# The channels of two SSD groups, projected ahead of the attention by seven products of quarters

## The chip, the cores and the metric

The kernel runs on one core of a Trainium2 chip. The metric is the device time of one execution in microseconds (us). Work is spread over five engines with queues of their own: PE multiplies matrices, ACT (ScalarE) evaluates functions and copies, DVE (VectorE) and POOL (GpSimd) do elementwise work, and SP issues most of the transfers between DRAM and on-chip memory. Each engine takes its instructions strictly in the order in which the program lists them, and waits by semaphores for the others.

## The reference

One layer of a hybrid decoder over 1024 tokens of width 1024, in float32 (cut to what matters here):

```python
h = rms_norm(x, norm_mix_g)
proj = h @ w_in                       # z 2048 | xbc 3072 | dt 32 | q_a 256 | kv_a 128 | k_rope 32 | gates 2048
xbc = silu(causal_depthwise_conv(xbc, conv_w, conv_b))     # 4 taps over the tokens
xs, bm, cm = split(xbc, [2048, 2048 + 4 * 128])            # xs, B and C: 4 groups each
dt = softplus(dt_raw + dt_bias)
y_ssd = rms_norm((ssd_chunked_scan(xs * dt, -dt * exp(a_log), bm, cm) + xs * d_skip) * silu(z)) @ w_ssd_proj
y_mla = mla(rms_norm(q_a), rms_norm(kv_a), k_rope) @ w_mla_proj        # 16 heads, causal
x = x + (sigmoid(g0) * y_ssd + sigmoid(g1) * y_mla) @ w_o
u = causal_depthwise_conv(rms_norm(x) @ w_up, conv_ffn_w, conv_ffn_b)  # 3 taps
x = x + (silu(u[:, :2816]) * u[:, 2816:]) @ w_down
```

## The kernel before

A float32 product is made of three matmuls on rounded parts: each operand is split into a high part and a remainder, and `mm3` (L173 to L177) issues high by high, high by low and low by high. So a step of 128 rows of the contraction costs three matmuls of 128x512, and a tile of 128 output columns for all 1024 tokens costs 2 halves x 8 steps x 3 = 48. The high part is cast by ACT, the remainder subtracted by DVE or POOL (`split`, `load_w`, L152 to L171).

The stages follow each other so:

- **Start.** For each half of 512 tokens, the normalised input is transposed in 8 blocks of 128 columns (`tps`), each split into an `h` tile (L263, L264), and multiplied by the 448 small columns (dt, q_a, kv_a, k_rope) into four banks `bl`, which are copied to `sm` (L417). Squares of q_a and kv_a are summed on ACT (L419, L420).
- **Into the attention.** Inverse roots of the means (`rsqrt_mean`, L114 to L125: small DVE operations, two chains), the scaling of `sm` (L433), six transposes of it into `qah`/`qal`/`kvh`/`kvl` (L442 to L447), the rotary tables on POOL (`tabs`, L451; `rq`/`rk`, L459 to L462; `krr`, L469 to L474), the softplus of dt (L480 on) and its running sums over the tokens (L502 to L522).
- **Attention**, four heads at a time. The order of PE is the order of the program, and its own products are short chains through DVE and ACT, so products that have nothing to do with it are put between: the list `background` holds generators, each of which yields once per step of three matmuls. `fill()` (L217) takes as many steps as the next character of the table `PACE` says. In the background are 16 gate tiles (`gate_tile`, stored to `g_d`) and 11 of the 16 z tiles (`z_tiles`, to `z_d`). `flush()` at the end runs what is left.
- **SSD**, four groups. A group's channels are 6 tiles: 4 of xs, one of B, one of C. `conv_tile` projects one with 48 matmuls, adds the 4 taps (one ACT operation, three DVE operations `L812` of 128x1024) and applies silu as tanh (L816, L817). Group 0 is projected alone (`conv_group(0)`); group g+1 fills the gaps of group g, `advance(n)` of 106 to 128 steps per group. A step of the scan is a chunk of 128 tokens: `xp`, `sp`, `yp`, `sn`.
- **Merge** with the gates, w_o, and the **MLP**. Its up projection works on pairs of column tiles: the 2 x 2 quarters (column tile by half of the contraction) against the 2 x 2 quarters of the activations (half of the contraction by half of the tokens) take seven products of sums of quarters in place of eight, of 4 steps each: 84 matmuls a pair and not 96. The sums of weight quarters are made on POOL (`w_sums`, L1149 to L1152), the casts on ACT, the remainders on POOL and DVE (L1141). The order in a pair is: `p5`, `p6`, `p7`, `p3`, `p4` and then `p12` of the next pair, 12 matmuls each and 24 in `p12`. `both_sums` (L1324, DVE) reads the bank of `p5` before `p3` accumulates onto it; it needs the copy of the bank of `p6` by ACT (L1318).

The tile framework releases on-chip memory by pools: the first user of a new pool over old memory waits for the last readers of the old one, transfers among them.

## Time and profile before

| | us |
|---|---|
| three runs | 2224.29, 2228.82, 2230.35: median 2228.82 |
| the profiled execution | 2224.44 |
| its span from the first to the last instruction | 2222.6 |
| PE busy in it | 2173.7 |
| end of the start (last `bl`) | 67.75 |
| first attention product (`s`) | 103.11 |
| attention's last store | 697.05 |
| group 0 projected alone | about 728 to 800 |

Marks of stages are read from the timeline. PE is the engine that is busy nearly always; matmuls overlap, so their pace is read from the distance of their starts and not from the duration of one. The mean granted TensorE clock is 0.996 of full speed.

### The profile page before, as it was taken

Reading aid. Unit: us, or ns where it says so; the run is one execution under the profiler, and the core shown is the slowest. Engines: PE = TensorE matmul, PEld = TensorE weight load, DVE = VectorE, ACT = ScalarE, POOL = GpSimd, SP = SyncE. Lnnn points to the kernel's source line nnn. Section 1 sums busy time; section 2 is a strip of 40 time slices with the busy share of each in tenths; the row PEclk is TensorE's granted clock in tenths of the full one; section 3 lists DMA queues with packets and bytes.
Section 4 is the critical chain, followed back from the end, with each engine's and each line's share of the span. In section 5 each row is a group of like instructions: output and inputs, shape, how many; then the busy total and the mean of one; then the engine's idle time right before and its main releaser. Section 6 shows DMA issues by size and latency. Waiting matters only on the chain.

```text
span 2222.6 us, 31323 instructions
## 1 busy us (share of the span) xinstructions
PE 2173.7 (98%) x11488; PEld 1765.2 (79%) x11488; DVE 1430.4 (64%) x2496; ACT 1012.4 (46%) x1852; POOL 822.4 (37%) x911
## 2 busy tenths in 40 slices
...
GB/s 146 54 68 49 40 48 63 50 45 39 69 43 130 68 76 152 181 162 167 95 227 207 178 223 203 166 162 95 67 95 86 81 81 86 76 142 246 201 130 67
DMA packets 112714, 253.57 MB, mean 114 GB/s; under 512 B 13168, under 2 KB 19248, under 8 KB 112560
## 3 DMA queue, kind: packets, MB, share of 16 engines
...
q8 instruction: 90, 1.47, 0.3%
q14 instruction: 64, 0.52, 0.1%
...
## 4 chain that ended last, share of the span: by engine, by line
PE 75%; DVE 13%; ACT 4%; DMA 3%; issue 2%; POOL 1%; SPq 0%; DVEq 0%; ACTq 0%; POOLq 0%
PE lin L175 12%; PE lin L177 12%; PE lin L176 12%; PE dps L177 8%; PE dps L175 8%; PE dps L176 8%; PE pv L670 2%; PE s L175 2%; PE s L176 1%; PE s L177 1%; PE s L627 1%; PE yp L891 1%; PE sn L874 1%; DMA wraw<-in_w_ssd 1%; DVE qk L588 1%
## 5 line engine op out<-in xcount | busy, mean ns | idle before, releaser
L175 PE MATMUL lin<-h,whi 128*128 128x512 f32 x1440 | 592.4, 411 | 0.0
L177 PE MATMUL lin<-h,wlo 128*128 128x512 f32 x1440 | 564.0, 392 | 0.0
L176 PE MATMUL lin<-h,whi 128*128 128x512 f32 x1440 | 563.0, 391 | 0.0
L175 PEld LDWEIGHTS lin<-h,whi 128*128 128x128 f32 x1440 | 271.4, 188 | 81.6 <-issue 33.4
L177 PEld LDWEIGHTS lin<-h,wlo 128*128 128x128 f32 x1440 | 270.7, 188 | 59.8 <-DVE wlo L154 0.2
L176 PEld LDWEIGHTS lin<-h,whi 128*128 128x128 f32 x1440 | 271.9, 189 | 53.2 <-issue 7.0
L153 ACT CAST whi<-wraw 128x512 fp32r<-128x512 f32 x276 | 166.6, 619 | 281.4 <-PE lin L176 131.6
L154 POOL TENSOR_TENSOR wlo<-wraw,whi 128x512 fp32r<-128x512 f32 x134 | 192.1, 1450 | 185.1 <-ACT whi L153 177.6
L659 ACT ACTIVATE e<-s 128x512 f32<-128x512 f32 (+1 forms) x192 | 93.7, 493 | 164.6 <-DVE s L657 137.7
L664 POOL TENSOR_TENSOR acc<-acc,e 128x512 f32<-128x512 f32 (+3 forms) x80 | 79.6, 995 | 230.8 <-ACT e L659 217.7
L154 DVE TENSOR_TENSOR wlo<-wraw,whi 128x512 fp32r<-128x512 f32 x142 | 99.2, 714 | 94.4 <-ACT whi L153 94.3
L154 DVE TENSOR_TENSOR h<-ar,h 128x1024 fp32r<-128x1024 f32 x40 | 48.7, 1225 | 108.8 <-ACT h L153 108.7
L850 ACT ACTIVATE seg<-abc,acum 128x128 f32<-128x128 f32 x256 | 80.6, 392 | 48.3 <-PE yp L891 42.3
L153 ACT CAST h<-ar 128x1024 fp32r<-128x1024 f32 x40 | 42.1, 1056 | 124.8 <-PE lin L176 115.7
L176 PE MATMUL dps<-wlo,h 128*128 128x512 f32 x240 | 93.4, 389 | 0.0
L175 PE MATMUL dps<-whi,h 128*128 128x512 f32 x240 | 93.4, 389 | 0.0
L177 PE MATMUL dps<-whi,h 128*128 128x512 f32 x240 | 93.4, 389 | 0.0
L812 DVE SCALAR_TENSOR_TENSOR xg<-craw,cl,xg 128x1024 f32<-128x1024 f32 x48 | 73.8, 1537 | 27.4 <-ACT xg L810 26.9
L664 DVE TENSOR_TENSOR acc<-acc,e 128x512 f32<-128x512 f32 (+3 forms) x80 | 53.5, 668 | 41.0 <-ACT e L659 40.4
L1140 ACT CAST xhi<-ur 128x512 fp32r<-128x512 f32 (+1 forms) x41 | 34.1, 832 | 89.5 <-PE dps L176 79.5
L670 PE MATMUL pv<-e,vt 128*64 128x512 f32 (+3 forms) x384 | 72.9, 499 | 0.0
L175 PE MATMUL s<-qh,kh 97*128 97x512 f32 (+1 forms) x192 | 68.5, 357 | 2.0 <-ACT qh L644 1.1
...
## 6 DMA issues: line engine op xcount, KB each, us to landing
wraw<-in_w_main SPq DMA_DIRECT2D x112, 256.0 KB, 3.1
ur<-in_w_up SPq DMA_DIRECT2D x44, 512.0 KB, 3.5
ar<-a_d SPq DMA_DIRECT2D x40, 512.0 KB, 5.1
abc<-ac_d POOLq DMA_DIRECT2D x32, 512.0 KB, 5.2
...
a_d<-uc SPq DMA_DIRECT2D x22, 512.0 KB, 2.6
...
```

Of the source, the lines that this page charges most:

```text
L153: S.copy(hi, raw)
L154: (eng or V).tensor_sub(lo, raw, hi.bitcast(F32))
L175: PE.matmul(ps, lhsT=ah, rhs=bh, start=first, stop=False, **more)
L176: PE.matmul(ps, lhsT=ah, rhs=bl, start=False, stop=False, **more)
L177: PE.matmul(ps, lhsT=al, rhs=bh, start=False, stop=last, **more)
L588: V.tensor_tensor(qk[:, :, 2 + hd, 0:64], qk[:, :, 2 + hd, 0:64], rr[:, :, 2 + hd:3 + hd].broadcast_to([P, 4, 64]), op=ALU.mult)
L659: S.activation(e[:, c0:512], ps[:, 0:w], AF.Exp)
L664: (V if hd else G).tensor_tensor(accs[hd][:, c0:512], accs[hd][:, c0:512], e[:, c0:512], op=ALU.add)
L670: PE.matmul(pv[hd * 64:(hd + 1) * 64, c0:512], lhsT=vt[:, j, hd * 64:(hd + 1) * 64], rhs=es[hd][:, c0:512], start=first, stop=last)
L812: V.scalar_tensor_tensor(c, raw[:, k:k + T], col(cw + k), c, op0=ALU.mult, op1=ALU.add)
L850: S.activation(seg[:, hd, :], abc[:, hd, :], AF.Relu, bias=acum[:, c, 8 * g + hd:8 * g + hd + 1], scale=-1.0)
L1140: S.copy(hi, r)
```

## The change

The 12 tiles of groups 0 and 1 (xs 0 to 7, B 0 and 1, C 0 and 1) are projected between the start and the attention, as six pairs of seven products, with the functions that served the MLP (moved to the top of the program, otherwise the same). The four combinations of activation quarters are made during the second half of the start and behind it (`job`). Each channel is convolved, silu is taken directly, and the result goes to `c_d` in DRAM; the SSD loads it (`channels`). Since the memory is tight, the first half's unsplit `h` (4 of 8 blocks) waits in `h_d` and is split again behind the last pair. The inverse roots, the scaling of `sm` and the softplus move into the gaps of the pairs. The 0.5 that served silu by tanh is now in the weights of the convolution, scaled for groups 2 and 3 behind the pairs. The background of the attention begins with 12 z tiles, then the 16 gates, and what is left of it when the attention ends fills the SSD; the head of `PACE` is shorter, and group 2 joins the fill of the first two groups. PE issues 72 fewer matmuls of 128x512 (7084 for 7156), and as many of every other shape as before. DVE has 61 more instructions, ACT 24 more (4 of them loads of function tables), POOL 15 more, SP 16 more transfers.

```diff
@@ PACE @@
-    "30030000000000000g080212018000011100522073110011303000010111011001011111000010000100001000002000"
+    "2222221116000011100522073110011303000010111011001011111000010000100001000002000"
...
+    c_d = dram.tile([24 * P, T], F32, name="c_d")
+    h_d = dram.tile([P, 4, 512], F32, name="h_d")
...
+    def w_sums(q, t=None):
+        q.s = t or pools["sum"].tile([P, KD, P], F32, name="us", bufs=1)
+        G.tensor_tensor(q.s[:, 0:4, :], q.r2[:, 0:4, :], q.r2[:, 4:8, :], op=ALU.add)
+        G.tensor_tensor(q.s[:, 4:8, :], q.s[:, 0:4, :], q.r1[:, 0:4, :], op=ALU.subtract)
+        G.tensor_tensor(q.r2[:, 0:4, :], q.r1[:, 0:4, :], q.r2[:, 0:4, :], op=ALU.subtract)
+        G.tensor_tensor(q.r1[:, 4:8, :], q.r1[:, 4:8, :], q.s[:, 4:8, :], op=ALU.subtract)
...
+    def product(ps, hl, c0, name, first, last):
+        hi, lo = hl
+        for i in range(4):
+            b = BQ[name][i]
+            mm3(ps, (hi[:, c0 + i, :], lo[:, c0 + i, :]), (b[:, 0, :], b[:, 1, :]), first and i == 0, last and i == 3,
+                skip_group_check=True)
+            yield True
+    def p12(q, x=None, y=None):
+        q.x = x or lin_tile()
+        q.y = y or banks_of[0]()
+        yield from product(q.x, q.a, 0, "11", True, True)
+        yield from product(q.y, q.a, 4, "21", True, True)
...
+    def p6(q, sums=True):
+        drain([product(q.x, q.b, 4, "t2", False, True)])
+        q.s2 = lt.tile([P, 512], F32, name="lt")
+        S.copy(q.s2, q.x)
+        if sums:
+            both_sums(q)
+    def both_sums(q):
+        q.q = lt.tile([P, 512], F32, name="lt")
+        V.tensor_tensor(q.q, q.z, q.s2, op=ALU.add)
+    def p7(q):
+        q.y = banks_of[0]()
+        drain([product(q.y, q.c, 0, "t3", True, True)])
...
-    background += [gate_tile(c) for c in range(16)] + [z_tiles(c) for c in range(11)]
+    background += [z_tiles(c) for c in range(12)] + [gate_tile(c) for c in range(16)]
...
+    cpairs = []
+    for a, c in ((16, 20), (0, 1), (2, 3), (17, 21), (4, 5), (6, 7)):
+        q = Pair()
+        q.pad, q.first, q.ct, q.src = 3, 1, (a, c), (w_main[16 + a], w_main[16 + c])
+        cpairs.append(q)
+    q = cpairs[0]
...
+                    if k == 5:
+                        nc.gpsimd.dma_start(out=h_d, in_=xb[0][:, :, 0:512])
+                else:
+                    if k == 0:
+                        q.s = quad_w()
+                        w_sums(q, q.s)
+                    n = k - 1
+                    if 0 <= n < 4:
+                        job("t1", n, b[1, n], act_tile(), b[0, n], b[1, n])
+                        job("t3", n, b[0, n], quad(), b[0, n + 4], b[0, n])
+                    elif n >= 4:
+                        V.tensor_tensor(b[1, n - 4], b[0, n], b[1, n - 4], op=ALU.subtract)
+                    if k == 3:
+                        w_second(q)
+                    if k > 3:
+                        small_squares(0, k - 4, 1)
                 if k:
-                    if half:
-                        fill()
                     small(half, k - 1, banks)
-            if half:
...
+    def channel(q, kind, u):
+        ct = q.ct[kind]
+        c = cb.tile([P, T], F32, name=f"uc{kind}")
+        cw = CG_CONVW + 4 * ct
+        S.activation(c, u[:, 3:T + 3], AF.Identity, bias=col(CG_CONVB + ct), scale=col(cw + 3))
+        for k in range(3):
+            V.scalar_tensor_tensor(c, u[:, k:k + T], col(cw + k), c, op0=ALU.mult, op1=ALU.add)
+        S.activation(c, c, AF.Silu)
+        nc.sync.dma_start(out=c_d[ct * P:(ct + 1) * P, :], in_=c)
...
+    for i in range(4):
+        job("t2", i, b[1, i], ca.tile([P, 2, 512], F32R, name="tb", bufs=4))
+    low()
+    q.x, q.y = lin_tile(), lin_tile()
+    drain([p12(q, q.x, q.y)])
+    first_sum(q)
+    w_third(q)
+    w_fourth(q)
+    for i in range(4):
+        job("t4", i, b[1, i + 4], quad(), b[1, i + 4], b[1, i])
+    low()
+    xctx.close()
+    cb = cvctx.enter_context(tc.tile_pool(name="cb", bufs=1))
...
+    for j, q in enumerate(cpairs):
+        nx = cpairs[j + 1] if j + 1 < len(cpairs) else None
+        if nx:
+            w_raw(nx)
+            w_first(nx)
+        p5(q)
+        if nx:
+            w_sums(nx)
+        p6(q)
+        if nx:
+            w_second(nx)
+        else:
+            for k in range(4):
+                raw = lt.tile([P, 512], F32, name="lt")
+                nc.sync.dma_start(out=raw.rearrange("p (i c) -> p i c", c=P), in_=h_d[:, :, k * P:(k + 1) * P])
+                h[0][k] = act_tile()
+                split(raw, h[0][k][:, 0, :], h[0][k][:, 1, :])
+        p7(q)
+        c22(q)
+        p3(q)
+        channel(q, 0, q.ug)
+        if nx:
+            w_fourth(nx)
+        p4(q)
+        c21(q)
+        channel(q, 1, q.uv)
+        if nx:
+            w_third(nx)
+            drain([p12(nx)])
+            c11(nx)
+        if j == 0:
+            name = last(mybir.EngineType.Activation)
+            small_squares(1, 0, 1)
+            tc.add_manual_dep(first_square[0], name, mybir.DependencyInfo(
+                mybir.DependencyClass.NoSync, mybir.DependencyReason.DATA), reason="order")
+            small_squares(1, 1, 3)
+        if j == 1:
+            rsqrt_mean(rr[:, 0, :], ss[:, 0, :], 256)
+            rsqrt_mean(rr[:, 1, :], ss[:, 1, :], 128)
+        if j == 2:
+            for half in range(2):
+                ts_ = slice(4 * half, 4 * half + 4)
+                V.tensor_tensor(sm[:, ts_, 32:288], sm[:, ts_, 32:288],
+                                rr[:, 0, ts_].unsqueeze(2).broadcast_to([P, 4, 256]), op=ALU.mult)
+                V.tensor_tensor(sm[:, ts_, 288:416], sm[:, ts_, 288:416],
+                                rr[:, 1, ts_].unsqueeze(2).broadcast_to([P, 4, 128]), op=ALU.mult)
+        if j == 3:
+            v, e, u = cdec, dte, acum
+            name = last(mybir.EngineType.DVE)
+            V.tensor_tensor(v, sm[:, :, 0:32], cl[:, CG_DTB:CG_DTB + 32].unsqueeze(1).broadcast_to([P, NT, 32]),
+                            op=ALU.add)
+            behind(name)
+            V.tensor_scalar(e, v, -1.0, None, op0=ALU.mult)
+            V.tensor_tensor(e, e, v, op=ALU.min)
...
+    G.tensor_scalar(cl[:, CG_CONVW:CG_CONVB + 24], cl[:, CG_CONVW:CG_CONVB + 24], 0.5, None, op0=ALU.mult)
...
         attention()
-        flush()
...
+        def channels(g):
+            chan[g] = dp.tile([P, 4, T], F32, name=f"xg{g % 2}", bufs=1)
+            for n in (16, 20):
+                chan[n + g] = dp.tile([P, T], F32, name="chan", bufs=4)
+            for half in range(2):
+                s = hs_(half)
+                for n in (16, 20):
+                    nc.sync.dma_start(out=chan[n + g][:, s], in_=c_d[(n + g) * P:(n + g + 1) * P, s])
+                nc.sync.dma_start(out=chan[g][:, :, s],
+                                  in_=c_d[4 * g * P:4 * (g + 1) * P, s].rearrange("(j p) t -> p j t", p=P))
...
+        channels(0)
         abc_load(0)
+        z_load(0)
         ls = dp.tile([P, P], F32, name="bt")
         lv = l_d.rearrange("r (c t) -> (r c) t", t=P)
-        for n, _ in enumerate(conv_group(0)):
-            if n == 17:
-                nc.sync.dma_start(out=ls, in_=lv)
-            if n == 33:
-                name = last(mybir.EngineType.DVE)
-                V.reciprocal(ls, ls)
-                behind(name)
-                nc.sync.dma_start(out=lv, in_=ls)
-        later()
-        z_load(0)
-        background.append(z_tiles(11))
+        nc.sync.dma_start(out=ls, in_=lv)
+        channels(1)
+        craws += [dp.tile([P, T + 3], F32, name="craw") for _ in range(2)]
+        for raw in craws:
+            G.memset(raw[:, 0:3], 0.0)
+        advance(12)
+        V.reciprocal(ls, ls)
+        advance(8)
+        nc.sync.dma_start(out=lv, in_=ls)
+        background += [z_tiles(12), z_tiles(13), conv_group(2)]
         fins = []
         for g in range(GROUPS):
-            if g + 1 < GROUPS:
-                background += [conv_group(g + 1), z_tiles(*((12,), (13,), (14, 15))[g])]
-            else:
+            if g == GROUPS - 2:
+                background += [conv_group(3), z_tiles(14, 15)]
+            if g == GROUPS - 1:
                 background += [mla_tiles()]
-            advance(8 if g else 14)
-            n = (106, 104, 128, 112)[g]
+            advance(8)
+            n = (96, 92, 128, 112)[g]
```

Three places show how the order moves. **First**, ACT at the second pair (`uc` is a channel, `us` and `ur` are sums and raw weights of a pair, `lt` a copy of a bank, `sm` the small columns). Before, the squares stood behind the start, among the gates:

```order
L419 ACTIVATE ljunk,lss<-sm 128x256
L420 ACTIVATE ljunk,lss<-sm 128x128
L292 ACTIVATE lt<-lin,hgb 128x512
L419 ACTIVATE ljunk,lss<-sm 128x256
L420 ACTIVATE ljunk,lss<-sm 128x128
L484 ACTIVATE de<-de 128x256
L153 CAST whi<-wraw 128x512
```

Now the second half's squares stand between the casts of the second pair and the copy that `both_sums` needs (the last row):

```order
L309 CAST whi<-us 128x1024
L309 CAST xhi_819<-ur_739 128x512
L309 CAST xhi_843<-ur_740 128x1024
L633 ACTIVATE uc_836<-row_736,cl 128x1024
L358 COPY lt<-lin 128x512
L491 ACTIVATE lt,lss<-sm 128x256
```

```order
L636 ACT_TABLE_LOAD
L636 ACTIVATE uc_812<-uc_812 128x1024
L493 ACTIVATE lt,lss<-sm 128x128
L491 ACTIVATE lt,lss<-sm 128x256
L493 ACTIVATE lt,lss<-sm 128x128
L491 ACTIVATE lt,lss<-sm 128x256
L493 ACTIVATE lt,lss<-sm 128x128
L309 CAST whi<-ur_888 128x1024
L636 ACTIVATE uc_836<-uc_836 128x1024
L309 CAST whi<-us 128x1024
L371 COPY lt<-lin 128x512
```

Eight squares, a table load and two silus have come in ahead of that copy.

**Second**, ACT's queue with the load of the rotary tables. Before, it was issued in the start:

```order
L153 CAST whi<-wraw 128x512
L263 ACTIVATE h<-tps,cl 128x512 x6
L451 DMA tabs<-in_cons 128x256
L497 ACTIVATE ea<-cl 128x32
L417 COPY sm<-bl 128x448
```

Now it is issued behind the last channel's silu:

```order
L758 ACTIVATE kvh<-tps,cl 128x512
L636 ACTIVATE uc_1586<-uc_1586 128x1024
L792 COPY acum<-tps 128x256
L763 DMA tabs<-in_cons 128x256
L796 COPY tot<-tps 128x256
```

Its memory lies over that of the channels, so it waits for the last two stores to `c_d` as well.

**Third**, SP behind the attention. Before:

```order
L681 DMA at_d<-ao 128x512
L685 DMA l_d<-e 4x256
L1070 DMA bt<-l_d 128x128
L988 DMA rb<-at_d 128x512
L307 DMA z_d<-lt 128x512
```

Now the loads of two groups' channels (6 MB) stand between the attention's last store and the next gate stores and weights:

```order
L967 DMA at_d<-ao 128x512
L971 DMA l_d<-e 4x256
L162 DMA wraw<-in_w_main 128x512
L1091 DMA chan<-c_d 128x512 x2
L1092 DMA xg_8312<-c_d 128x4x512
L1091 DMA chan<-c_d 128x512 x2
L1092 DMA xg_8312<-c_d 128x4x512
L1364 DMA bt<-l_d 128x128
L1091 DMA chan<-c_d 128x512 x2
L1092 DMA xg_8327<-c_d 128x4x512
```

```order
L1091 DMA chan<-c_d 128x512 x2
L1092 DMA xg_8327<-c_d 128x4x512
L430 DMA g_d<-lt 128x512 x3
L1373 DMA l_d<-bt 128x128
L162 DMA wraw<-in_w_main 128x512
```

The stores of gates and the weights of the next tile are now behind twelve loads.

391 lines of the change are left out of this document (196 added, 195 removed).

## The prediction

> **What bounds the kernel now.** First the page: busy times, and the shares of the chain that ended last.
>
> ```profile
> PE 2173.7 (98%) x11488; PEld 1765.2 (79%) x11488; DVE 1430.4 (64%) x2496; ACT 1012.4 (46%) x1852; POOL 822.4 (37%) x911
> PE 75%; DVE 13%; ACT 4%; DMA 3%; issue 2%; POOL 1%; SPq 0%; DVEq 0%; ACTq 0%; POOLq 0%
> ```
>
> PE is busy for 2173.7 of 2222.6 us, so only about 49 us of waiting is left, and a matmul less is worth its pace wherever PE doesn't wait. Next the view of windows (us from the start, busy time with the number of instructions of PE, its weight loads, DVE, ACT and POOL, then granted clock, DMA share and GB/s), for the stages that the change touches.
>
> ```profile
> 30.00:60.00 30.00, 30.00 (x163) 27.06 (x162) 9.33 (x14) 15.88 (x37) 8.11 (x9) 1.00 0.17 53
> 60.00:90.00 30.00, 26.91 (x124) 22.83 (x123) 20.43 (x55) 10.99 (x31) 9.04 (x16) 0.94 0.13 42
> 704.00:712.00 8.00, 8.00 (x37) 6.60 (x37) 0.69 (x1) 5.46 (x14) 3.07 (x3) 1.00 0.98 356
> 728.00:800.00 72.00, 72.00 (x320) 59.60 (x319) 33.95 (x27) 27.36 (x39) 17.53 (x14) 1.00 0.21 64
> ```
>
> Group 0's projection alone (728 to 800) has no idle time: moving it saves no wait there, only the matmuls that it drops. The start is full too (30 to 60). What waits is the way into the attention (60 to 90, clock 0.94). Its timeline on PE (start, duration, instruction, idle time before it):
>
> ```profile
> 67.75 0.39 PE L175 MATMUL lin<-h,whi 128*128 128x512 f32 x1
> ...
> 78.43 0.39 PE L177 MATMUL lin<-h,wlo 128*128 128x512 f32 x1
> 81.91 1.94 PE L442 MATMUL tps<-cn,sm 128*128 128x128 f32 x8 [3.09 <-DVE rsa L123]
> 83.50 0.78 PE L175 MATMUL lin<-h,whi 128*128 128x512 f32 x1
> 84.92 0.42 PE L175 MATMUL lin<-h,whi 128*128 128x512 f32 x1
> ...
> 103.11 0.25 PE L175 MATMUL s<-wqh,qah 128*128 128x192 f32 x1
> ```
>
> The 48 starts from 67.75 to 78.43 give the pace: 10.68 / 47 = 0.2272 us a matmul. Then PE waits 3.09 us for the inverse roots, and what follows is slow: the three matmuls from 83.50 to 84.92 take 1.42 us and not 0.68, and the eight transposes before them 1.59. About 1.5 us is lost to the clock on top of the wait. From 67.75 to the first `s` at 103.11 are 35.4 us; the 114 background matmuls in it (25.9 us at the pace) and its transposes and sums (some 4 us) leave about 5.4 us of stall in all.
>
> **The sum, part by part.** It is made against the profiled execution, 2224.44 us, which lies at the low end of the three runs and 4.4 below their median.
>
> *Matmuls dropped.* 72 x 0.2272 = **-16.4**. The pairs of the MLP show what seven products cost with their surroundings; the issues of its weight loads are one pair apart:
>
> ```profile
> 1727.75 4.45 SPq L1127 DMA_DIRECT2D ur<-in_w_up  x2
> 1747.02 4.45 SPq L1127 DMA_DIRECT2D ur<-in_w_up  x2
> ```
>
> 19.27 us for 84 matmuls, where the pace gives 19.08. So 6 x 0.2 = **+1.1**, if the six new pairs run like those. They differ in three things: three convolution taps and not two, chains of the attention put between, and a first pair whose operands are just being made. For these I need durations (groups by line; the number behind the bar is busy us, then mean ns):
>
> ```profile
> L1141 POOL TENSOR_TENSOR wlo<-us,whi 128x1024 fp32r<-128x1024 f32 x19 | 47.5, 2498 | 13.1 <-ACT whi L1140 13.1
> L1149 POOL TENSOR_TENSOR us<-ur 128x512 f32<-128x512 f32 x21 | 29.4, 1400 | 54.8 <-DMA ur<-in_w_up 53.3
> L1151 POOL TENSOR_TENSOR ur<-ur,ur 128x512 f32<-128x512 f32 x22 | 32.3, 1470 | 0.0
> L1152 POOL TENSOR_TENSOR ur<-ur,us 128x512 f32<-128x512 f32 x21 | 44.8, 2132 | 2.7 <-DVE h L1141 1.2
> L154 DVE TENSOR_TENSOR h<-lt,h 128x512 fp32r<-128x512 f32 x16 | 10.7, 688 | 4.5 <-ACT h L153 4.5
> L1141 DVE TENSOR_TENSOR xlo<-ur,xhi 128x512 fp32r<-128x512 f32 x21 | 34.9, 1660 | 0.0
> L1141 DVE TENSOR_TENSOR xlo<-ur,xhi 128x1024 fp32r<-128x1024 f32 x20 | 25.3, 1263 | 0.0
> L1344 DVE SCALAR_TENSOR_TENSOR uc<-uv,cl,uc 128x1024 f32<-128x1024 f32 x44 | 58.9, 1339 | 1.2 <-ACT uc L1342 0.4
> L812 DVE SCALAR_TENSOR_TENSOR xg<-craw,cl,xg 128x1024 f32<-128x1024 f32 x48 | 73.8, 1537 | 27.4 <-ACT xg L810 26.9
> L433 DVE TENSOR_TENSOR sm<-sm,lrr 128x1024 f32<-128x1024 f32 x2 | 2.4, 1218 | 0.0
> L486 DVE RECIPROCAL du<-du 128x256 f32<-128x256 f32 x1 | 1.8, 1753 | 0.0
> L1140 ACT CAST whi<-us 128x1024 fp32r<-128x1024 f32 x21 | 22.2, 1055 | 82.1 <-PE lin L176 79.2 <-POOL us L1150 2.9
> L1342 ACT ACTIVATE uc<-uv,cl 128x1024 f32<-128x1024 f32 x22 | 27.5, 1250 | 18.0 <-DVE uv L1359 14.2 <-DVE uc L1363 3.8
> L1353 ACT ACTIVATE uc<-uc 128x1024 f32<-128x1024 f32 x22 | 23.4, 1064 | 2.1 <-DVE uc L1344 2.1
> L1353 ACT ACT_TABLE_LOAD x1 | 1.3, 1283 | 0.0
> ```
>
> *Second half of the start.* It loses its fill, and DVE gets four more operations of 0.69 in each of four blocks, some 3.5 us with the block's own remainder, where PE has 12 matmuls and 4 transposes, about 2.9. Nothing (the operations lag behind without hurting) to 4 (DVE slowed by POOL's sums beside it, as in the 1.66 of a 128x512 against 0.69); I take **+2**.
>
> *Hand-over from the first pair to the second.* Count from S, the end of the start. DVE has nine remainders, four differences and the first pair's two weight remainders to do: 9 x 0.69 + 4 x 0.69 + 1.26 + 0.69 = 10.9, and is through at about S+12.4 with the casts ahead. Only then is the memory of `xt` free, and the raw weights of the second pair can be loaded. Loads and stores take:
>
> ```profile
> ur<-in_w_up SPq DMA_DIRECT2D x44, 512.0 KB, 3.5
> a_d<-uc SPq DMA_DIRECT2D x22, 512.0 KB, 2.6
> ```
>
> The load lands at 15.9, the cast ends at 17.0, POOL's remainder at 19.4, its four sums (1.40, 1.40, 1.47, 2.13) at 25.8, the remainder of the sums at 28.3. PE, with 108 matmuls from S on, wants that remainder at about 25. So it waits 3.3, and by the 3.09 us wait above loses 1.6 more to the clock: **+4.9**, between 3 (the fourth sum at the 1.40 of the first, and no loss of clock) and 6 (two of DVE's remainders at 1.66).
>
> By the Trainium skill, "TensorE: Matmul & The Clock Gate", Part 1, the clock falls only after an idle window of about 3.4 us, in a window that runs freely; the trace has it lower after 3.09 us, so I keep the row. By the page's length alone this term would be 3.3.
>
> *`both_sums` of the second pair.* The lateness goes on along ACT: its cast of `ur` waits for the fourth sum (25.8); what follows is in the order of the first place above. A token tile's two squares take 0.71, the distance of these two starts:
>
> ```profile
> 68.21 0.42 ACT L419 ACTIVATE ljunk<-sm 128x256 f32<-128x256 f32 x1
> ...
> 68.92 0.52 ACT L417 COPY sm<-bl 128x448 f32<-128x448 f32 x1
> ```
>
> Half a cast (0.62), a cast 1.06, Identity 1.25, a copy 0.6, eight squares 2.84, the table load 1.28, silu 1.06, cast 1.06, silu 1.06 make 10.8, so S+36.6. Cast 1.06 and copy 0.6 make 38.3, and DVE, through with the inverse roots by then, adds the two banks (0.69) by 39.0. `p3`, which overwrites the bank, is up at 25 + 3.3 + 8.2 = 36.5. 2.5 late; DVE's taps between can add to it; with the 1.5 for the clock **+4**, between 1 and 7.
>
> By the Trainium skill, "ScalarE: Activation LUTs", What ACT_TABLE_LOAD costs, a switch of tables is 1.28 us and as much again of drain, 2.66 in all. The row here has 1.283, and the ACTIVATE behind it in the trace starts at once. By the page this term would be 1.4 larger, and the next as well.
>
> *Pairs three to six.* Chains stand ahead of `both_sums` on DVE: the rest of the inverse roots and 3.8 us of scaling, and at the fifth pair the softplus: table load 1.28 and Exp on ACT ahead of the copy, reciprocal 1.75 on DVE. The slack of `both_sums` is small: `p5` to `p7` are 8.2 us, in which DVE also has three taps (4.0) and two sums. Stalls of 0.3 to 2.4 us came out, in sum 5 or so if all are real, 0 if DVE catches up; **+3**.
>
> *Into the attention.* The rotary tables no longer lie under the start. Their durations, and the step from the store of the sums to `s`, before:
>
> ```profile
> 65.21 0.42 POOL L459 TENSOR_TENSOR rq<-tabs,cl 128x128 f32<-128x128 f32 x1 [17.51 <-DMA tabs<-in_cons]
> 67.87 0.42 POOL L462 TENSOR_TENSOR rk<-tabs,cl 128x128 f32<-128x128 f32 x1
> 69.58 0.46 POOL L469 TENSOR_TENSOR krr<-sm,rk 128x128 f32<-128x128 f32 x1 [1.28 <-ACT sm L417]
> 72.49 0.47 POOL L474 TENSOR_TENSOR krr<-krr,krtmp 128x128 f32<-128x128 f32 x1
> 98.42 0.32 SPq L522 DMA_DIRECT2D ac_d<-act__900  x1
> 100.52 0.11 POOL L554 MEMSET qk<- 128x8 f32 x1 [22.54 <-DMA ac_d<-act__900]
> 101.75 1.72 POOL L154 TENSOR_TENSOR wql<-wraw,wqh 128x384 fp32r<-128x384 f32 x2 [1.01 <-ACT wqh L153]
> ```
>
> Count from E, the end of the last pair's `p4`. DVE has three taps and three remainders of `h` ahead of the last sum, so that is done at 5.9, Identity at 7.2, three taps with four remainders of q and kv between at 13.1, silu at 14.2, its store (2.6) at 16.8, the table load (2.1, as `ac_d`) at 19, eight tables (65.21 to 68.29) at 22.1, `krr` (69.58 to 72.96) at 25.5. `wqh` waits for it, and from cast to the first `s` are 103.11 - 100.5 = 2.6: E+28. PE's own work, 63 matmuls, transposes and sums, is 18.3. The stall of 9.8 with 1.5 for the clock stands against 5.4 before: up to 6; since part of it is waited for piecemeal, I take **+5**, from 2 to 9.
>
> *Start of the SSD.* 6.3 MB of channels at the 356 GB/s that the queue reached (704 to 712) are 18 us; with the issue and what else runs, 20 to 23. The next weights and the gates' stores stand behind. The 20 steps of background (13.6 us) and the first group's own matmuls hide most of it: **+2**, from 0 to 7.
>
> *Everything else* is as before: the attention has the same products, the MLP the same code. The first group's fill has no convolution, which spares DVE, and at the beginning of the second group one chunk has only 12 filling matmuls where others have 36; I set these against each other. The added stores to `c_d` (12 x 512 KB) go out under PE's work at 0.13 to 0.2 DMA share.
>
> Sum: -16.4 + 1.1 + 2 + 4.9 + 4 + 3 + 5 + 2 = **+5.6**. With the bounds low -16.4 + 1.1 + 0 + 3 + 1 + 0 + 2 + 0 = -9; high -16.4 + 1.1 + 4 + 6 + 7 + 6 + 9 + 7 = +24.
>
> **Rivals.** (a) *The cover holds.* For it: the MLP loop has the same order and no idle time, and DVE and ACT are at 64% and 46%. Then of the stalls only the start and a part of the way into the attention stay, -16.4 + 1.1 + 2 + 2 = -11: 2218. Against it: the dependence of the second pair's load on `xt`, and of `krr` on the last stores, is in the program, and nothing of the MLP has it. (b) *Slower for good*: the chain store, `tabs`, tables, `krr`, `wqh` is priced in full (11.3 against 5.4) and the load of the channels holds up the first weights of the SSD by 7; it decides once DVE's taps at the end of the pairs take the 1.54 us that they take in the SSD under POOL's load and not 1.34. With the other terms as above: 5.6 + 1 + 5 = +12, 2240. (c) *It doesn't do what it says*: the 72 matmuls go, but at the pace of the clock in the stalled stretches the pairs show no gain over plain projection, and the rest is hidden; about 0, 2229.
>
> **How the numbers follow.** What can be told from no change here is about 0.3%, 6.7 us. The forecast, a few us more than before, gets 0.5, (a) 0.22, (b) 0.18, (c) 0.1. Applied to the median of the runs, 2228.8 + 5.6 = **2234**. The range takes in the lows of (a) and the middle of the high bounds: 2216 to 2248. Faster by over 0.3%: nearly all of (a) and a little else, 0.22. Slower: (b) and four tenths of the forecast, 0.38. The rest, 0.40, is within.
>
> **What would show it.** In the changed kernel's profile: a wait of PE of about 3 us at the second pair's `p5` for POOL's remainder of `us`, one as long at its `p3` for DVE's `lt`, and 8 to 10 us before the first `s`, with `krr` on POOL ending last and `tabs` landing behind the last `c_d`; lower clock in those windows; pairs three to six at 19.3 to 21 us; gate stores late by some us after the attention. It is wrong if the six pairs run at 19.3 us from the first on, or if the tables are done before PE asks for `wqh`: then it is (a). It is wrong the other way if SSD groups 0 and 1 take longer than before by more than their fill says.

## The result, and the profile after

The kernel after takes 2301.89 us (median of four runs, 2299.33 to 2305.14), the kernel before on the same chip 2229.59: ratio 1.0328, 95% interval 1.0303 to 1.0352. Its profiled execution has a span of 2298.8 us, 76.2 more than before. From its page, the busy times and the shares of the chain that ended last:

```profile
PE 2192.3 (95%) x11416; PEld 1765.6 (77%) x11416; DVE 1487.5 (65%) x2561; ACT 1037.9 (45%) x1880; POOL 854.9 (37%) x926
PE 69%; DVE 15%; ACT 5%; DMA 5%; issue 4%; POOL 2%; SPq 0%; ACTq 0%; POOLq 0%; DVEq 0%
```

PE has fewer instructions and yet is busy 18.6 us longer, and it sits idle for 2298.8 - 2192.3 = 106.5 us, where it was 48.9. To see where, both traces are cut at the same marks: the last `bl`, the first `s`, the attention's last store, the first and the last `xp` of the scan, and the first store to `a_d`. The view of windows of the kernel before (columns as in the prediction):

```profile
0.00:67.50 67.50, 57.22 (x289) 49.67 (x290) 27.44 (x52) 32.85 (x68) 17.90 (x26) 0.97 0.34 122
67.50:103.10 35.60, 32.49 (x153) 26.45 (x152) 23.29 (x63) 15.38 (x37) 8.32 (x17) 0.95 0.16 52
103.10:697.00 593.90, 580.14 (x3274) 446.48 (x3272) 380.37 (x1040) 287.09 (x646) 241.69 (x393) 1.00 0.16 52
697.00:801.80 104.80, 104.80 (x463) 86.72 (x464) 38.61 (x33) 41.65 (x70) 26.94 (x26) 1.00 0.32 105
801.80:1244.80 443.00, 437.75 (x2659) 351.18 (x2658) 366.14 (x569) 255.51 (x492) 255.09 (x237) 1.00 0.50 163
1244.80:1603.80 359.00, 347.75 (x1982) 301.29 (x1980) 222.31 (x396) 150.16 (x280) 68.21 (x70) 1.00 0.49 159
1603.80:2222.60 618.80, 613.60 (x2676) 503.41 (x2676) 372.23 (x345) 229.73 (x262) 204.28 (x147) 1.00 0.34 117
```

And of the kernel after:

```profile
0.00:72.20 72.20, 54.94 (x271) 45.92 (x272) 42.60 (x72) 45.91 (x87) 21.82 (x21) 0.98 0.34 127
72.20:242.80 170.60, 144.68 (x605) 114.77 (x605) 129.93 (x158) 78.63 (x113) 77.02 (x55) 0.94 0.24 84
242.80:856.20 613.40, 591.05 (x3273) 450.45 (x3274) 386.04 (x1047) 285.69 (x645) 237.16 (x392) 0.99 0.15 50
856.20:875.50 19.30, 19.29 (x84) 15.59 (x85) 0.00 (x0) 10.46 (x26) 7.61 (x11) 1.00 0.79 274
875.50:1315.60 440.10, 417.09 (x2530) 332.36 (x2529) 336.05 (x546) 238.09 (x472) 240.78 (x232) 0.97 0.56 181
1315.60:1678.80 363.20, 349.74 (x1982) 302.33 (x1980) 222.46 (x396) 149.69 (x280) 68.08 (x70) 0.99 0.48 157
1678.80:2298.80 620.00, 615.47 (x2676) 504.17 (x2676) 370.44 (x345) 229.47 (x262) 202.43 (x147) 0.99 0.34 117
```

Work was moved from one stage to another, so the time of a stage alone says little. I call **excess** what a stage takes more than before, less 0.2272 us for each PE instruction that it has more. (The counts differ by 75 in sum and not by the 72 of the pages, since a matmul that lies across a cut counts on both sides of it.)

| stage | us before | us after | PE instructions more | excess |
|---|---|---|---|---|
| start | 67.5 | 72.2 | -18 | +8.8 |
| pairs, into the attention | 35.6 | 170.6 | +452 | +32.3 |
| attention | 593.9 | 613.4 | -1 | +19.7 |
| to the first `xp` | 104.8 | 19.3 | -379 | +0.6 |
| scan | 443.0 | 440.1 | -129 | +26.4 |
| merge | 359.0 | 363.2 | 0 | +4.2 |
| MLP | 618.8 | 620.0 | 0 | +1.2 |
| sum | 2222.6 | 2298.8 | -75 | +93.2 |

93.2 - 75 x 0.2272 = 76.2, the difference of the spans. The same cut of the runs below shows how far single executions scatter: with the same code, the start took 72.1 to 75.3 us and the merge 358.7 to 363.3 (the kernel before among them), so 3 us of a stage mean nothing by themselves. The scan, with the code of the kernel after, took 435.3 to 441.8; the stage of the pairs, whose runs with unchanged code agree within 1 us, scatters less. So the 4.2 of the merge isn't taken for an effect of the change. The costliest waits of PE in the kernel after (engine, line and releaser; us in total, times, longest):

```profile
PE cb L177 <- DVE lt L377: 17.3, 5, 9.3
PE sn L1169 <- DVE bt L1158: 13.6, 5, 4.2
...
PE xp L1135 <- DVE xg L1112: 7.3, 1, 7.3
...
PE s L177 <- ACT wqh L155: 3.5, 1, 3.5
...
```

`cb` <- `lt` is `p3` waiting for `both_sums`; `sn` and `xp` are the scan. Besides 8.9 us for the first load, of which the kernel before has 8.8, these three are the largest, and all wait for DVE, which is busy for only 65% of the span.

**The pairs**, cut at the `p3` of each (windows, the second to the last):

```profile
100.70:119.90 19.20, 9.88 (x35) 7.38 (x35) 18.86 (x24) 9.37 (x24) 14.89 (x7) 0.79 0.34 109
119.90:143.30 23.40, 22.17 (x85) 17.71 (x85) 20.00 (x26) 9.24 (x10) 11.07 (x6) 0.88 0.25 91
143.30:163.80 20.50, 19.43 (x85) 15.66 (x85) 14.97 (x13) 9.12 (x10) 11.99 (x7) 1.00 0.29 103
163.80:186.90 23.10, 19.45 (x85) 15.68 (x85) 19.34 (x20) 10.81 (x12) 12.39 (x7) 1.00 0.12 46
186.90:209.90 23.00, 21.05 (x84) 16.83 (x84) 20.18 (x27) 10.60 (x13) 7.00 (x5) 0.93 0.14 46
```

A pair takes 23.4, 20.5, 23.1, 23.0 us. Plain projection of it would be 96 x 0.2272 = 21.8: the seven products gained nothing here. In front of the second `p3` DVE is busy for 18.86 of 19.20 us. Its timeline there:

```profile
103.36 2.30 DVE L635 SCALAR_TENSOR_TENSOR uc<-row,cl,uc 128x1024 f32<-128x1024 f32 x1
105.58 2.32 DVE L310 TENSOR_TENSOR xlo<-ur,xhi 128x1024 fp32r<-128x1024 f32 x1
107.82 3.45 DVE L635 SCALAR_TENSOR_TENSOR uc<-row,cl,uc 128x1024 f32<-128x1024 f32 x1
...
115.60 2.33 DVE L127 SCALAR_TENSOR_TENSOR lrr<-rsa,lrr 128x8 f32<-128x8 f32 x1
...
117.97 1.23 DVE L705 TENSOR_TENSOR sm<-sm,lrr 128x1024 f32<-128x1024 f32 x1
119.11 0.68 DVE L377 TENSOR_TENSOR lt<-cb,lt 128x512 f32<-128x512 f32 x1
```

and POOL's beside it:

```profile
102.43 2.15 POOL L319 TENSOR_TENSOR us<-us,ur 128x512 f32<-128x512 f32 x1
104.53 2.29 POOL L320 TENSOR_TENSOR ur<-ur,ur 128x512 f32<-128x512 f32 x1
107.70 2.48 POOL L310 TENSOR_TENSOR wlo<-ur,whi 128x1024 fp32r<-128x1024 f32 x1 [0.89 <-ACT whi L309]
...
115.57 2.34 POOL L310 TENSOR_TENSOR wlo<-us,whi 128x1024 fp32r<-128x1024 f32 x1 [3.18 <-ACT whi L309]
```

The last row of DVE is `both_sums`; it ends at 119.79, and `p3` starts at 119.85. The durations ahead of it depend on POOL. The operation on 128x8 at 115.60, whose like take 0.17 us when alone, ends at 117.93: with POOL's remainder (115.57 + 2.34 = 117.91). The tap at 107.82 takes 3.45; from the end of POOL's remainder, 110.18, it is 1.1. The tap at 103.36 and the remainder at 105.58 end 1.1 us behind POOL's sums (104.58, 106.82). So each of these operations, started while POOL's ran, seems to have begun its work only when that had ended. The count over the stage says the same: of its 36 taps 23 begin while no elementwise operation of POOL runs and take 1.27 to 1.29 us, and 13 begin beside one and take 1.28 to 3.46, 2.36 in the mean; in the MLP only 9 of 88 begin beside one. By the Trainium skill, "SBUF — State Buffer", Who interferes with whom, a DVE operation with two inputs from SBUF (the on-chip memory that isn't the banks of PE's sums) and a POOL operation that reads it exclude each other for the whole instruction, and the one issued second waits; the trace agrees, with these four ends, and `both_sums`, which reads one input from a bank, took 0.68 us while a sum of POOL's ran (117.99 to 120.34).

### The profile page after: what moved, and what is told of

The parts are those of the page before. It is cut to its first block, busy times and chain, and to the rows that moved or that the text cites. A ratio compares the mean times of both kernels' runs of the same rounds, so it can differ in the third digit from the quotient of the medians.

```text
span 2298.8 us, 31401 instructions
## 1 busy us (share of the span) xinstructions
PE 2192.3 (95%) x11416; PEld 1765.6 (77%) x11416; DVE 1487.5 (65%) x2561; ACT 1037.9 (45%) x1880; POOL 854.9 (37%) x926
## 4 chain that ended last, share of the span: by engine, by line
PE 69%; DVE 15%; ACT 5%; DMA 5%; issue 4%; POOL 2%; SPq 0%; ACTq 0%; POOLq 0%; DVEq 0%
PE lin L177 10%; PE lin L178 10%; PE lin L179 10%; PE dps L177 8%; PE dps L179 8%; PE dps L178 8%; PE pv L956 2%; DVE uc L635 2%; PE s L177 1%; PE s L178 1%; PE s L179 1%; PE s L913 1%; DMA wraw<-in_w_ssd 1%; PE yp L1186 1%; DVE xg L1107 1%
## 5 line engine op out<-in xcount | busy, mean ns | idle before, releaser
L177 PE MATMUL lin<-h,whi 128*128 128x512 f32 x1276 | 531.8, 417 | 3.0 <-ACT lt L429 2.1
L179 PE MATMUL lin<-h,wlo 128*128 128x512 f32 x1276 | 502.1, 393 | 0.0
L178 PE MATMUL lin<-h,whi 128*128 128x512 f32 x1276 | 501.7, 393 | 0.0
L177 PEld LDWEIGHTS lin<-h,whi 128*128 128x128 f32 x1276 | 242.0, 190 | 81.7 <-issue 35.8
L179 PEld LDWEIGHTS lin<-h,wlo 128*128 128x128 f32 x1276 | 241.1, 189 | 53.8 <-DVE wlo L156 0.2
L178 PEld LDWEIGHTS lin<-h,whi 128*128 128x128 f32 x1276 | 242.5, 190 | 47.7 <-issue 7.3
L155 ACT CAST whi<-wraw 128x512 fp32r<-128x512 f32 x252 | 151.1, 618 | 244.1 <-PE lin L178 91.3
L156 POOL TENSOR_TENSOR wlo<-wraw,whi 128x512 fp32r<-128x512 f32 x110 | 161.6, 1484 | 102.0 <-ACT whi L155 101.8
L945 ACT ACTIVATE e<-s 128x512 f32<-128x512 f32 (+1 forms) x192 | 93.6, 492 | 179.6 <-DVE s L943 148.0
L156 DVE TENSOR_TENSOR h<-ar,h 128x1024 fp32r<-128x1024 f32 x40 | 48.9, 1225 | 108.8 <-ACT h L155 108.6
L309 ACT CAST xhi<-ur 128x512 fp32r<-128x512 f32 (+1 forms) x51 | 42.3, 831 | 116.3 <-PE dps L178 85.4
L915 DVE CUSTOM_DVE_ANT_0 s<-s,negw 128x128 f32<-128x128 f32 (+3 forms) x128 | 62.2, 495 | 18.0 <-PE s L913 17.8
L310 POOL TENSOR_TENSOR wlo<-ur,whi 128x1024 fp32r<-128x1024 f32 x24 | 61.4, 2557 | 33.5 <-ACT whi L309 28.7
```

The source lines that it names most:

```text
L155: S.copy(hi, raw)
L156: (eng or V).tensor_sub(lo, raw, hi.bitcast(F32))
L177: PE.matmul(ps, lhsT=ah, rhs=bh, start=first, stop=False, **more)
L178: PE.matmul(ps, lhsT=ah, rhs=bl, start=False, stop=False, **more)
L179: PE.matmul(ps, lhsT=al, rhs=bh, start=False, stop=last, **more)
L310: eng.tensor_sub(lo, r, hi.bitcast(F32))
```

## The experiments

Each kernel is the kernel after with one edit, unless said otherwise. A time without a ratio is that of a single run. The kernel before took 2220.75 to 2230.03 (medians) beside them.

### The stage of the pairs

**Taps left out.** The three convolution taps of the twelve early channels are not computed (the output is then of other numbers).

```diff
         S.activation(c, u[:, 3:T + 3], AF.Identity, bias=col(CG_CONVB + ct), scale=col(cw + 3))
-        for k in range(3):
-            V.scalar_tensor_tensor(c, u[:, k:k + T], col(cw + k), c, op0=ALU.mult, op1=ALU.add)
```

> The three taps of the twelve early channels are left out (36 operations of DVE, 60 us of its time): the convolution there is one tap. In the changed kernel the pairs from the second on take 20.5 to 23.4 us from `p3` to `p3`, where 84 matmuls at the pace are 19.1. Theory C (DVE, slowed by POOL's sums beside its taps, is what `both_sums` waits for): all pairs from the third on run at 19.1 to 19.6, and the stage from the end of the start to the first `s` falls from 170 to 140 to 150 us. Theory D (the chains put between and ACT's casts, not the taps): they stay above 20.5, and the stage stays above 160.

2278.94 us; the stage takes 151.5 in place of 170.6, its excess falls from 32.3 to 13.2. The waits for `lt` are 9.6 us in two places and no longer 17.3 in five; 7.2 of it remains at the second pair. That lies between the two theories: from the second `p3` on a pair takes 21.0, 19.2, 21.8 and 20.7 us, so one alone runs at the 19.1 to 19.6 of theory C.

**POOL's sums left out.** The four sums of weight quarters of pairs two to six are left out, and a raw quarter stands for them (other numbers again).

```diff
     def w_sums(q, t=None):
+        if q.pad == 3 and t is None:
+            q.s = q.r2
+            return
```

> POOL's four sums of weight quarters are left out for the second to the sixth pair (36 us of POOL); the products take the raw weights, so the channels of these pairs are not what they should be. All 36 taps on DVE stay (60 us, 1.67 each). Theory I (POOL and DVE hinder each other when both read two operands from on-chip memory): the taps fall to 1.27 to 1.35 each though nothing was taken from DVE, and the waits of 1.2, 1.1, 3.7 and 2.0 at the third to the sixth pair's `p3` fall below 0.7. Theory J (DVE simply has too much in the pair): the taps stay near 1.6 and those waits stay.

2287.75; the stage 162.2, excess 23.9. The taps are shorter. The group of the taps in this stage (busy, mean ns), first after, then here:

```profile
L635 DVE SCALAR_TENSOR_TENSOR uc<-row,cl,uc 128x1024 f32<-128x1024 f32 x36 | 59.8, 1669 | 3.7 <-ACT uc L633 3.5
```

```profile
L638 DVE SCALAR_TENSOR_TENSOR uc<-row,cl,uc 128x1024 f32<-128x1024 f32 x36 | 56.1, 1566 | 2.2 <-ACT uc L636 2.0
```

POOL's remainders are still there, and a tap still takes 1.566 and not the 1.34 of the MLP. By its signs this is theory J: the taps stay near 1.6, and the waits at the third to the sixth `p3` are little smaller (1.08, 0.69, 3.27, 1.86, where they were 1.23, 1.07, 3.65, 1.99). From the first `p3` to the second it took 26.2 us in place of 33.7 (86.1 to 119.85 after), from the second to the sixth 89.1 in place of 90.1. So nearly all of the gain lies ahead of the second `p3`, where the sums also stand in the chain behind the late load.

**Both left out.**

> Left out: the three taps of the twelve early channels, and the four sums of weight quarters of pairs two to six (so these products are of other numbers). Apart, the one cut the stretch from the last bl to the first s by 19 us and the other by 8, from 170.6. Theory J (two causes that add: DVE's queue with the taps in it, and POOL's four sums, which make DVE and themselves slow): 143 to 146 us. Rival K (one cause seen twice, DVE's lateness: the sums matter only because they slow the taps): 150 to 152, as without the taps alone. If it is below 140, what is left against 125.6 is small and the pairs' whole loss is DVE's and POOL's; above 146, a part of it is in ACT's queue (casts, silus, table loads) or in the chains of the attention.

The comparison value 125.6 in this text (and the 47 us in the text on the run with all edits, below) rests on a count of mine, 396 more instructions, that the windows correct to 452: even with the kernel before is 35.6 + 452 x 0.2272 = 138.3. The stage took 148.0:

```profile
74.70:222.70 148.00, 139.12 (x607) 112.79 (x605) 74.31 (x122) 78.55 (x113) 36.84 (x36) 0.97 0.28 97
```

Excess 9.3. Left out together they are worth 23.0, and apart 19.1 + 8.4 = 27.5: partly one cause seen twice, so neither of the two theories is right as it stood. 9.3 remain; `p3` still waits 7.0 us in two places, 4.7 at the second pair and 2.4 at the fifth. So 23 of 32 us are the taps and POOL's sums. The taps act in the whole stage (with both left out, 83.3 us from the second `p3` to the sixth; without the taps alone 82.8), the sums ahead of the second `p3`; whether they do it there by slowing DVE or by their place in the chain, these runs don't separate.

**Chains one pair later**, so that the inverse roots don't stand ahead of the second pair's `both_sums`: the four conditions `j == 0, 1, 2, 3` become `j == 1, 2, 3, 4`.

> The squares, the inverse roots, the scaling and the softplus each move one pair later (squares and roots out of the second pair; scaling and softplus into the fifth and sixth). Theory H: the wait of 9.3 at the second pair's `p3` falls below 4, and a wait of some 3 to 5 comes up in the third; the stage shrinks by 3 to 8. Theory G: the 9.3 stays above 7, and the stage does not shrink, since the third pair gets the chains on top.

2302.51; the stage 173.7, excess 35.2. The wait of 9.32 became 6.24, and the third pair's 1.23 became 8.84; a new one of 4.2 stands before the transposes of `sm`. From the second `p3` to the sixth it took 96.1 us, 6.0 more, and ahead of the second 30.8, 2.9 less. The lateness only moved along: the wait is not below the 4 of theory H, and the stage did not shrink, as G has it.

**All chains behind the last pair**: each condition becomes `j == 5`.

> All four chains (second squares, inverse roots, scaling, softplus) stand behind the last pair, where the kernel before had them behind the start; nothing is left out. Theory M (what is put between the pairs sets most of their waits): the waits at `p3` of the second, fifth and sixth pair fall to 6 (the late load's share), 1.5 and 1.5, from the second pair's `p3` (119.9 in the changed kernel) to the sixth's (209.9) are 82 to 85 us and not 90, and the chains' 10 to 14 us come back ahead of the first `s`: the stage is 168 to 178. Theory N (three taps a channel set the pairs' pace): the pairs keep 20.5 to 23, 88 to 91 us in all.

2309.16; excess 45.1. The waits of PE in that stage:

```profile
PE tps L754 <- DVE sm L705: 18.6, 1, 18.6
PE cb L177 <- DVE lt L377: 9.2, 5, 6.2
PE tps L791 <- DVE cdec L733: 6.5, 1, 6.5
```

Without chains between them the last pairs come every 19.7 to 20.6 us, with waits of 1.05 at most at a `p3`; the second still waits 6.2. From the second `p3` to the sixth it is 83.1 us, as theory M has it (82 to 85), while the stage is 12.8 longer than after, beyond M's 178. What was saved stands in full before the transposes, and more. In waits, the chains cost 17.3 - 9.2 = 8.1 us where they were put, and 18.6 + 6.5 = 25.1 behind.

**Raw weights early.** The two halves of `xt` get pools of their own; the second pair's weights are loaded into the first half's memory at once.

```diff
-    xpool = xctx.enter_context(tc.tile_pool(name="xp", bufs=2, side="right"))
+    xp1 = xctx.enter_context(tc.tile_pool(name="xp1", bufs=1, side="right"))
+    xp0 = x0ctx.enter_context(tc.tile_pool(name="xp0", bufs=1, side="right"))
...
+    x0ctx.close()
+    pools["raw"] = cvctx.enter_context(tc.tile_pool(name="cr", bufs=1))
+    w_raw(cpairs[1])
```

> The two halves of `xt` lie in pools of their own, so that the raw weights of the second pair come into the first half's memory as soon as its last reader is through, some 8 us earlier than behind the second half's remainders. In the changed kernel PE waits 2.9 for POOL's remainder of the second pair and 9.3 at its `p3`. Theory G (the load is the root of both): the first wait goes and the second falls to 5 or less; the stage from the end of the start to the first `s` (170.6) shrinks by 6 to 10. Theory H (the squares and the inverse roots put into the second pair are the root of the 9.3): the first wait goes, the second stays at 8 to 12, and the stage shrinks by 0 to 4.

2297.93; excess 29.7. The wait of 2.92 for POOL's remainder is gone, so the dependence on `xt` was real; but the first `p3` now waits 5.46 and the second 7.83. POOL's sums now run beside DVE while the first pair's own operands are made, which is a likely cause and not tested. The stage shrank by less than 4 us, as theory H has it.

**Rotary tables early.** The load, and the half of the tables that `krr` needs, stand at the end of the pairs, in memory of the `lt` ring, ahead of the last stores to `c_d`.

```diff
+    tabs = lt.tile([P, 512], F32, name="lt")
+    nc.sync.dma_start(out=tabs[:, 0:256], in_=cons[:, NCON:NCON + 256])
...
+    rope_table(rk, CG_KR)
     cvctx.close()
...
-    tabs = bq.tile([P, 256], F32, name="tabs")
-    nc.scalar.dma_start(out=tabs, in_=cons[:, NCON:NCON + 256])
```

> The rotary tables are loaded and the half of them that `krr` needs is made during the last pair, in memory that the channels don't hold, and the conversion of the taps' weights stands behind them. Theory K (the chain store, load of the tables, tables, `krr` sets the first `s`): the wait of 3.5 us ahead of the first `s` goes, and from the last pair's `p3` (209.9 in the changed kernel) to the first `s` (242.8) are 26 to 29 us and not 32.9. Theory L (the last channel's taps and their store set it, or `ac_d`): 31 to 33.

2303.29; the wait before the first `s` falls from 3.54 to 0.60, and from the last `p3` to `s` it takes 29.6 in place of 32.9; the stage's excess is 28.9. So the chain of theory K was the link that waited, though 29.6 lies just above its 29. In the whole it doesn't show: the attention took 615.6 in this run and 613.4 after.

### The attention

PE's own products there and the number of its instructions are as before. Two things differ: at which step of a background tile the table's large and small fills fall, and what kind of tile (z or gate) runs first.

**Eight more steps of fill before the first `s`.**

```diff
-    "2222221116000011100522
+    "222222111e000011100522
```

> One character of the fill table: the fill ahead of the last block of the running sums takes 14 steps and not 6, so that 28 background steps are done at the first attention product where the changed kernel had 20 and the kernel before 44. 28 and 44 stand at the same place of a 16-step tile. In the changed kernel the attention, from the first `s` to the last store of `at_d`, took 242.8 to 856.2, 613.4 us; before 593.9. Theory A (the fill table was fitted to where tiles begin and end; the 8 steps' shift moves weight casts, remainders and stores to other places in the heads' chains): the attention falls to 594 to 602. Theory B (it is the kind of tile, z with its work on DVE standing ahead of the gates): it stays at 610 to 616. Either way the wait ahead of the first `s` shrinks by up to 5.5 us (24 matmuls at 0.2272), and the SSD has 8 steps fewer to fill with.

**Gates first**, then z tiles, as before the change (and with them the order of halves in the first tile).

```diff
-    background += [z_tiles(c) for c in range(12)] + [gate_tile(c) for c in range(16)]
+    background += [gate_tile(c) for c in range(16)] + [z_tiles(c) for c in range(12)]
```

> The background begins with the 16 gates again, then the 12 z tiles, at the same counts of steps. Theory A (place of the tiles' ends): the attention stays at 608 to 618 us. Theory B (kind of tile): it falls to 594 to 602. Total by A 2296 to 2306, by B 2282 to 2290.

**Both**, with the early tables and the early weights:

> The edits that helped a stage, together: gates first, 8 more steps of fill ahead of the first `s`, the tables early, the early load of the second pair's weights. Theory A and B together (both the place and the kind of background tiles matter): the attention takes 592 to 598. If one edit had only done what the other does: 602 to 605. Total by the first 2270 to 2280, by the second 2280 to 2288; against the kernel before 1.02 to 1.03.

The attention in the eight steps' run, in the gates' run and in the run with both:

```profile
248.30:850.90 602.60, 585.99 (x3274) 449.98 (x3273) 379.25 (x1045) 286.49 (x646) 239.42 (x393) 0.99 0.16 51
```

```profile
247.90:851.60 603.70, 587.87 (x3273) 449.46 (x3274) 381.28 (x1038) 287.08 (x645) 236.81 (x392) 0.99 0.15 50
```

```profile
248.10:842.40 594.30, 582.44 (x3274) 450.10 (x3274) 375.85 (x1038) 286.02 (x644) 237.75 (x391) 0.99 0.15 51
```

613.4 became 602.6 and 603.7 with one and 594.3 with both, the 593.9 of the kernel before. Each theory alone was half right. The early tables and weights have no part in it: in the eleven other runs whose attention is filled as in the kernel after, these two edits alone among them (615.6 and 612.0), it took 612.0 to 615.8 us. So the attention's +19.7 is all in the phase and the kind of what fills it. Its waits in the kernel after are many and short (the longest behind the first `s` 2.90), and the clock adds to them: it was granted at half for 16.0 us of this stage, and never before the change. Idle time there grew by 8.6 us and busy time by 10.9, of which the half clock can be at most 8.0. Which of ACT's or DVE's operations meet badly in it I haven't taken apart. The run with both took 2280.98 (four runs), ratio 1.0242, interval 1.0225 to 1.0259; the gates alone 2291.38. The eight steps have a price: they are 24 matmuls fewer to fill the scan with, whose excess rose to 35.6 in that run (26.4 after); the run took 2295.58 in the whole, for 2301.89, which a single run doesn't set clear of the scatter.

### The scan

At its start, SP's queue and DVE's (issues with their duration; `bt` is here the small tile of the sums):

```profile
863.89 3.29 SPq L1364 DMA_DIRECT2D bt<-l_d  x1
...
879.45 1.27 SPq L430 DMA_DIRECT2D g_d<-lt  x3
```

```profile
879.75 0.95 DVE L1371 RECIPROCAL bt<-bt 128x128 f32<-128x128 f32 x1 [24.37 <-DMA bt<-l_d]
880.62 1.16 DVE L1162 TENSOR_TENSOR abc<-abc,chan 128x1024 f32<-128x1024 f32 x1
...
883.09 0.28 DVE L1158 COPY bt<-sp 128x128 f32<-128x128 f32 x1
```

The 64 KB of the sums are issued behind 3 MB of channels and land 16 us later. Their reciprocal heads DVE's queue, DVE stands still for 24.37 us, and everything that the first chunk needs comes after it.

**Sums first, and less fill in group 0.** The sums' load is issued ahead of the channels, and 24 steps of fill are moved out of group 0, 12 of them to group 1.

```diff
+        nc.sync.dma_start(out=ls, in_=lv)
         channels(0)
...
-            n = (96, 92, 128, 112)[g]
+            n = (72, 104, 128, 112)[g]
```

> In the SSD the load of the softmax sums stands ahead of the channel loads, and group 0 takes 72 steps of fill and not 96, group 1 104 and not 92. In the changed kernel the scan, from its first `xp` to the last, takes 440 us with waits of 4.2, 2.1, 4.2, 7.3 and 4.2. Theory E (the sums' load lies behind 3 MB of channels and its reciprocal blocks DVE; group 1 has no fill until group 0 is finished and all the convolutions): the first wait goes and those of 4.2 and 7.3 in group 1 fall to 2 or less, the scan takes 424 to 432. Theory F (the transfers' rate sets the start, and DVE is full in group 1 whatever the fill): the waits only move, 436 to 444.

2308.40, the scan 450.5: worse, and beyond both theories. The sums were in time and the wait of 4.22 for them at 883 is gone, but the next gate store and the weights still stood behind 6 MB of channels (waits of 6.00, 2.95 and 2.61 at 891 to 904): the excess of the first half of group 0 is 17.7, and 9.8 in the kernel after. Since the fill was changed too, this run doesn't price the early load of the sums by itself.

**Sums first, second group's channels late**: fills as they were, and `channels(1)` is issued in the third chunk of group 0.

```diff
+        nc.sync.dma_start(out=ls, in_=lv)
         channels(0)
...
-        channels(1)
...
+                if g == 0 and u == 6:
+                    channels(1)
```

> The load of the softmax sums stands first behind the attention, and the channels of group 1 (3 MB) are loaded during the third chunk of group 0 and not with those of group 0. Theory E2 (6 MB in one piece hold up the first weights, gates' stores and the reciprocal): the first scan stage's waits (4.2 and 2.1 in the changed kernel) fall to 2 in sum, with no new ones at 891 to 904, and the scan takes 428 to 434 us for 440. Theory F2 (3 MB are enough to hold them up, the rest of the scan is bound by DVE): 436 to 444.

2293.73, the scan 430.1, excess 16.2: 10 us gained, as theory E2 has it, all in the first half of group 0, whose excess goes from 9.8 to 0.5. They come with both loads moved; what each is worth isn't separated. Its waits are now:

```profile
PE sn L1169 <- DVE bt L1158: 8.5, 5, 4.2
PE xp L1135 <- DVE xg L1112: 7.3, 1, 7.3
```

**z 13 behind the convolution of group 2**, beside the edit just shown: `background += [z_tiles(12), conv_group(2), z_tiles(13)]`.

> The edit of the run with the late second load (the sums' load first, the second group's channels loaded during the first group's scan), and beside it one more move in the list of background work: the tile z 13 goes behind the convolution of group 2 and no longer ahead of it. Theory G (the convolution of group 2 is the last item in the list, so that the flush at the end of group 1 ends with its last channel and PE must wait for copy, taps and tanh of it before the first xp of group 2): the wait of 7.31 us for xg before that xp goes or falls below 1.5 us, with about 1.5 us of lost clock behind it, so the stretch from the first xp to the last is 430.1 - 8.5 = about 421.5 us, if nothing starts to wait in its place. Rival H (DVE is simply full in groups 0 and 1, and whatever stands last waits as long): 4 to 7 us of wait show up at another place there, and the stretch stays between 427 and 432.

2286.72 (two runs), ratio 1.0262, interval 1.0242 to 1.0283. The scan takes 427.1, excess 13.2. The wait for `xg` is gone, as the first theory has it, but 3.0 us came out and not 8.5, no more than the scan scatters with the same code: at the start of group 1 waits of 3.21 and 2.18 came up, as the rival has it. DVE is busy for 91 and 93% of the two halves of group 1.

**Taps of group 2 left out as well** (other numbers).

> The kernel with the late second load and z 13 behind the convolution of group 2, in which the three taps of the six channels of group 2 are left out as well (the output is then of other numbers). It takes 18 operations of about 1.5 us, 27 us, from DVE between the end of group 0 and the start of group 2, where DVE is busy 91 to 97% of the time. There the scan loses 8.4 + 3.0 us more than its dropped matmuls say, with 7.8 us of waits. Theory H (DVE is full in that stretch, because the convolution of group 2 is all in the scan of group 1, and its queue is late whichever item stands last): these waits fall to below 2 us and the stretch from the first xp to the last to 427 - 9 = 418 us, with 414 to 421. Rival L (it is the order alone: PE meets the end of a tile, or the norm of group 0's output, at a bad place, whatever DVE has to do): the waits of 3.2 and 2.2 us behind the first chunk of group 1 stay, and the stretch is 423 to 428.

```profile
875.10:1292.70 417.60, 409.64 (x2530) 327.97 (x2529) 306.95 (x527) 238.13 (x472) 227.21 (x232) 0.99 0.59 191
```

417.6, the number of theory H, excess 3.9. Of the waits at the start of group 1, 2.2 for DVE and 2.2 for ACT's `seg` remain, where H expected under 2: a part may be the order. So 13.2 - 3.9 = 9.3 of the scan's 26.4 us are the taps of group 2. They were little heavier than in the kernel before (31.7 us of DVE for 29.0), but they were elsewhere: before, group 0's fill held the convolution of group 1 (DVE busy 0.76 and 0.96 of its two halves) and group 1's that of group 2 (0.87, 0.95); after, group 0 has none or little (0.46, 0.65), and group 1 all of it (0.95, 0.97), with the norm of group 0's output.

### All that gained, and one edit of the kernel before

> All that gained so far in one kernel: gates ahead of the z tiles, the eight more steps of fill before the first s, tables early, raw weights of the second pair early, the sums' load first, the second group's channels late, and z 13 behind the convolution of group 2. If the losses of the attention and of the scan have separate causes, as the runs say, the gains add: 2281 - 10 (the start of the scan) - 8.5 (theory G) = about 2262, attention near 594 and scan near 420. By rival H 2271. Neither reaches the kernel before (2227): what is then left is the stage of the pairs, 172.9 us where 35.6 + 396 x 0.2272 = 125.6 would be even with the kernel before, 47 us.

2273.49 (four runs), ratio 1.0204, interval 1.0187 to 1.0222; the scan 428.2, the attention 592.7. That is close to rival H's 2271. In its profiled execution start and pairs keep an excess of 11.7 and 29.1, the scan 19.7, and 71 fewer matmuls by the windows' counts give 16.1 back. No version reached the kernel before.

**The wait of 3.09 us in the kernel before.** The softplus is ordered behind the scaling in DVE's queue (`scaled` is DVE's last instruction of it), so that the inverse roots come earlier.

```diff
+    behind(scaled)
```

> The kernel before, with one order added: the softplus begins behind the scaling of the small columns, so that the inverse roots run without it between them. The wait of 3.09 us ahead of the first `tps` from `sm`, and the slow matmuls behind it (about 1.5), should go: 2220 to 2225 for 2229, a ratio of 0.997 to 0.999. If the softplus then comes late for the running sums, a wait of 1 to 4 appears there and it is even.

2228.03 (twelve runs) against 2226.71 (seventeen), ratio 1.0006, interval 0.9998 to 1.0015: no change. The wait of 3.09 is gone, one of 3.33 stands some 9 us later. The way into the attention took 36.1 us for 35.6: it seems to be as long as its chain, whichever link waits.

## Why the prediction was wrong

It said 2234, in 2216 to 2248, and the kernel took 2301.89. Step by step:

- **Matmuls dropped, -16.4**: they went (72 by the pages).
- **Second half of the start, +2** (0 to 4): 8.8, and 9 to 12 in the runs with the same start. The step counted DVE's operations. PE waits as much for ACT, whose casts of the new combinations stand ahead of those of `h`, and then for DVE:

```profile
58.05 0.47 PE L177 MATMUL bl<-shi,h 128*128 128x448 f32 x1 [1.25 <-ACT h L566]
59.42 0.47 PE L179 MATMUL bl<-shi,h 128*128 128x448 f32 x1 [0.69 <-DVE h L568]
```

- **Hand-over, a wait of 3.3**: 2.92 at 100.68, for POOL's remainder, behind the load that waits for `xt`, and half clock for 3.41 us after it. Right in place, cause and size.
- **`both_sums` of the second pair, 2.5 late**: 9.32 late. The place is right and the chain isn't. The step followed ACT and took DVE to be through; DVE was the late one (ACT's silu waits 5.88 for a tap), because the taps and remainders beside POOL take 2.3 to 3.5 us in place of the MLP's 1.3, and because inverse roots and scaling had come ahead of `both_sums` (with the chains moved away 6.24 remain, without the taps 7.18). The kernel before shows the same wait, which the prediction passed over when it said that the MLP loop has no idle time; the line below is its PE at the `p3` of the MLP's second pair. The 19.27 us of a pair were read 120 us further on, where the loop runs without such a wait.

```profile
1604.35 0.79 PE L175 MATMUL dps<-h,xhi 128*128 128x512 f32 x1 [6.46 <-DVE lt L1324]
```

- **Pairs three to six, +3, and the pace, +1.1**: from the second `p3` to the sixth 90.1 us, where 4 x 19.27 = 77.1 was the basis: +13.0. The condition "if the six new pairs run like those" failed, and "0 if DVE catches up" with it: DVE didn't. Left out or moved behind, the taps were worth 7.3 of the 13.0, the chains 7.0 and POOL's sums 1.0, each by itself. (The sum of the high bounds takes 6 for this term, where its own text has 5.)
- **Into the attention, +5**: E + 28 was forecast for the first `s`. E was 217.15 (the last `p4` ran partly at half clock), and `s` came at E + 25.7. The chain is right: the tables began at E + 18.9, where 19 was forecast, and `krr` on POOL ended last, at 242.20. The sizes are not: from there to `s` it took 0.6 us and not 2.6, and PE waited 5.7 in sum, 3.54 of it before `s`, where 9.8 was forecast. Hand-over, `both_sums`, pairs, pace and this step made 4.9 + 4 + 3 + 1.1 + 5 = 18.0; the stage's excess is 32.3.
- **Start of the SSD, +2** (0 to 7): 10. The loads were counted, and what stood behind them was looked for among weights and gate stores. The largest wait there, 4.22 us, was for the small load of the sums, whose reciprocal holds up DVE, and that link was missing; but with this load first and 6 MB behind it (and less fill) the weights and gate stores waited more, so the record gives the 10 only to both moves together.
- **Everything else, 0**: the step that failed. Of the 70.6 us by which the spans' difference of 76.2 exceeds the forecast of 5.6, 42.1 are here: the attention's 19.7, 16.4 of the scan and 6.0 of small remainders. The attention's +19.7 comes from the same products with another fill between them, and of the scan 9.3 us from the taps bunched into group 1; 3.0 more may come from the convolution's place at the end of the list. "I set these against each other" is an average over two groups; the second one was full.

The clock is the part that none of these steps had in full: idle time grew by 57.6 us, and the other 35.6 of the 93.2 of excess are busy time beyond the pace. At most 30 of these are matmuls at a lower clock (0.983 granted of 2298.8 us and 0.996 of 2222.6, which are 39.1 and 8.9 us lost, idle time included); the rest isn't explained. Of the rivals, (c) had one thing right, the pairs without a gain, but at the wrong price, and (b) named the taps at 1.54 under POOL's load (1.67 came) and gave them 1 us. The sentence on what would make it wrong the other way, SSD groups longer than their fill says, is what happened.

What stays open: the 9.3 us of the pairs without taps and sums (waits of 4.7 and 2.4, and their clock), the 3.9 of the scan (less than its scatter), what the small load and the bulk loads each cost at its start, the causes within the start's 8.8 beyond the waits shown, and which operations meet in the attention when the fill is shifted.
